# Weights alone on SP's queue behind the first phase, other loads and stores issued by GpSimd

## The chip, the cores and the metric

The kernel runs on one core of a Trainium2 chip. The metric is the device time of the run in microseconds; three runs gave a median of 2641.81 us (2640.67 to 2645.19). One further run was taken with the hardware profiler, and every row quoted below is from it.

## The reference

The reference is a two-layer streaming encoder for one sequence of 512 tokens with 2048 channels, all in float32: first an mLSTM layer (8 heads, key width 256, value width 512), then a layer of banded attention (16 heads of 128) whose keys and values are computed once from the stream between the layers. Both layers are conditioned by a vector c: `sc` is silu(c), and each layer's shift, scale and gate are its product with a matrix of 2048 by 6144, one sum over 2048 entries for each channel.

```python
sc = silu(c)
for l in range(2):
    mod = sc @ ada_w[l] + ada_b[l]
    shift, scale, gate = split(mod, 3)
    h = rmsnorm(x, g_pre[l]) * (1 + scale) + shift
    if l == 0:
        y = mlstm_mixer(h, a_w_in, a_conv_w, a_conv_b, a_gate_b, a_g_head, a_w_out)
    else:
        kmod = sc @ kv_ada_w + kv_ada_b
        hkv = rmsnorm(x, kv_g) * (1 + kmod[D:]) + kmod[:D]
        k, v = split(hkv @ kv_w, 2)
        y = band_attention_mixer(h, k, v, b_w_in, b_rel, b_w_out)
    x = x + gate * rmsnorm(y, g_post[l])
return x
```

Each mixer ends with a product with an output matrix (4096 by 2048 in layer 1, 2048 by 2048 in layer 2).

## The kernel before

Every product of float32 matrices is done as three matmuls (`mm3`, `mm` at L316): both operands are split into a rounded part and a remainder. Activations stay in SBUF as such pairs; weights pass through once. A weight piece is 512 KB in the order in which TensorE needs it. `raw_load` (L260) issues its DMA from SP into one of three slots (`wr`), `wpiece` takes it, ScalarE rounds it into `wh` and VectorE subtracts (`split`, both L244); when VectorE is done the slot is free for the piece three further on. Some pieces also get sums (`ws`, L283 to 285) for products that save a matmul in eight.

The conditioning vectors are not made on TensorE. `ada_load` (L549) brings 128 rows of the transposed matrix (1 MB, or halves of 512 KB) into a slot `ada`, and `ada_sum` (L555) lets VectorE multiply by `sc` and sum along the row into a column of `mod`. They are spread over the kernel: `ada_start` in the first phase (SP), `background` under the mLSTM heads (already issued by GpSimd), `whole_load` under the out-projection of layer 1 (two slots, 1 MB each), `scale_load` (L1226, L1228: tiles `scQ` and `adq`, quarters) under the key projection, `gate_sums` under the out-projection of layer 2 (four slots, half rows).

The stages in order of time: a first phase (input norm, first projections, conditioning sums); gate rows of the mLSTM and eight heads (`ps_qk`, `ps_v`, `ps_o`, `ps_z`; each head loads its rows `nm` and `ssum` from `gsc`, L912 and L913, and stores its output in `ysc`, L1016); the out-projection of layer 1 (`yr` L1067 and L1075, `ps_y_True` and `ps_y_False`, residual rows `xr` L1132 and `xsc` L1141); the normed stream (`nsc`, L1174); the values (`ps_kv`, stores `vsc` L1302 and L1374, each of 512 rows of 512 bytes); the keys (`ksc`, L1366); queries; attention by head (`kt`, `vt` L1394, `bias` L1419, `y2c` L1474); and the out-projection of layer 2 (`y2r` L1529, `ps_y`, tail from about 2500 us), with squares for the output norm (`sqy`, L1116), evictions (`yo`, L1113), the gate columns (`ggd`, stored at L829 and read back as a row at L1105), residuals (`x2`, L1519) and the stores of the result by `finish` (L1543).

`kept` (L1192) loads a normed row (`xt`) back from `nsc` for the sums `hs` and `h2s` that the key and query projections use.

A scheduler with a model of the engines puts each engine's instructions in one order ahead of time, and each engine then runs its queue strictly in that order; an instruction that waits for a semaphore holds everything behind it on that engine, DMA issues included. `pin` keeps calls in the order of the program, and `high_priority` moves some ahead. Before the change SP issues the weights' 537 DMAs and beside them nearly all other loads and stores, GpSimd 57 `ada` loads.

Of the kernel before, what the change touches and what calls it, by code (L numbers as in the profile page):

```python
# [15 lines left out]
P = 128  # L16
D = 2048
S = 512
KT = D // P
# [170 lines left out]
def hybrid_trunk(ctx, tc, xT, xN, c, adaT, cols, wst, wg, ext, kc, out):  # L190
# [351 lines left out]
    def ada_load(i, p, n, pin=lambda ins: ins, parts=1, js=None, queue=nc.sync):  # L542
# [28 lines left out]
    def ada_start(k):  # L571
        return [ada_load(KT + k, ap_, 2, pin), ada_load(k, sp, 2, pin)]
# [14 lines left out]
    early = [ada_load(KT, ap_, 2, pin, 2), ada_load(0, sp, 2, pin, 2)]  # L587
# [98 lines left out]
    def background(n):  # L686
# [4 lines left out]
        while pending and len(loaded) < 3:  # L691
            p, bufs = (bp, 1) if len(pending) % 3 == 1 else (ap_, 2)
            loaded.append(ada_load(pending.pop(0), p, bufs, pin, queue=nc.gpsimd))
# [49 lines left out]
    nc.sync.dma_start(maskd, kc[:, 144:272])  # L743
    graw = tp.tile([P, KT, 16], F32, tag="t", name="graw")
    gw = hp.tile([P, KT, 32], F32R, tag="p0", name="gw")
    nc.sync.dma_start(graw, wg)
# [3 lines left out]
    def gates():  # L750
# [28 lines left out]
        nc.sync.dma_start(gsc[0], on)  # L779
        nc.vector.tensor_tensor(w, u, w, op=ALU.add)  # L780
        nc.scalar.activation(w, w, AF.Exp, scale=-1.0)
        nc.sync.dma_start(gsc[1], w)
# [36 lines left out]
    def gates_out(layer, k0, k1, pl, **kw):  # L819
# [9 lines left out]
        nc.sync.dma_start(ggd[layer, k0:k1], row)  # L829
# [49 lines left out]
    for h in range(NH):  # L879
# [32 lines left out]
        nc.sync.dma_start(nm, gsc[0, h].partition_broadcast(P))  # L912
        nc.sync.dma_start(em, gsc[1, h].partition_broadcast(P))  # L913
# [22 lines left out]
        for i in (2 * h, 2 * h + 1):  # L936
            pin(nc.sync.dma_start(bsc[i], ext[i].partition_broadcast(P)))
# [76 lines left out]
        for i in range(4):  # L1014
            nc.vector.tensor_tensor(so[i], so[i], dd, op=ALU.mult)
            nc.sync.dma_start(ysc[h, :, i, :], so[i])  # L1016
# [23 lines left out]
    def whole_load(bufs=2):  # L1040

        if not scC:
            scC.append(cp.tile([P, D], F32, tag="sc", name=f"scC{whole[0]}"))
            pin(nc.sync.dma_start(scC[0], csc[0].partition_broadcast(P)))
# [15 lines left out]
    def y_tile(k):  # L1060
        while len(ys) <= k:
            n = len(ys)
            h, q = divmod(n // 2, 2)
            with tc.high_priority(AHEAD):
                if n < 4:
                    raw = wp.tile([P, 2, S], F32, tag="raw", name=f"yr{h}_{q}", bufs=RAW_BUFS)
                    nc.sync.dma_start(raw, ysc[h, :, 2 * q : 2 * q + 2, :])  # L1067
                    raw = [raw[:, j, :] for j in range(2)]
                else:
# [4 lines left out]
                    for j in range(2):  # L1074
                        nc.sync.dma_start(raw[j], ysc[h, :, 2 * q + j, :])  # L1075
# [27 lines left out]
    def gate_row(layer, g, gb=ssum):  # L1103

        nc.sync.dma_start(gb, ggd[layer, 4 * g : 4 * g + 4, :].rearrange("k p -> (k p)").partition_broadcast(P))  # L1105
# [22 lines left out]
    def fetch_xr(m, n):  # L1128

        for g in range(len(xrs[m]), len(xrs[m]) + n):  # L1130
            xrs[m].append(xr_p.tile([P, S], F32, tag="xr", name=f"xr{m}_{g}"))
            nc.sync.dma_start(xrs[m][g], xN[m, :, g * S : (g + 1) * S])  # L1132

    def residual(m):
        rs = row_rstd(m)
        for g in range(4):
# [4 lines left out]
            nc.sync.dma_start(xsc[m, :, d], y)  # L1141
# [10 lines left out]
    def turned(pair, gs, use):  # L1152
# [3 lines left out]
        for g in gs:  # L1156
# [5 lines left out]
            for kk in range(2):  # L1162
# [11 lines left out]
                nc.sync.dma_start(nsc[k : k + 2, :, t].rearrange("a p t -> p a t"), keep)  # L1174
# [14 lines left out]
    def kept(k, t):  # L1189
        w = t.stop - t.start  # L1190
        tmp = tp.tile([P, S], F32, tag="t", name=f"xt{k}_{t.start}")[:, :w]
        nc.sync.dma_start(tmp, nsc[k, :, t])  # L1192
# [27 lines left out]
    def scale_load():  # L1220

        for i, j in scale_cols[:2]:
            d = slice(j * S, (j + 1) * S)
            if j not in scQ:
                scQ[j] = cp.tile([P, S], F32, tag="sc", name=f"scQ{j}_{i}", bufs=2)
                pin(nc.sync.dma_start(scQ[j], csc[0, d].partition_broadcast(P)))  # L1226
            a = cp.tile([P, S], F32, tag="adq", name=f"adq{i}_{j}", bufs=4)
            pin(nc.sync.dma_start(a, adaT[i, :, d]))  # L1228
# [61 lines left out]
    def values(g, ms, at={}):  # L1290
        pv = [newp(f"ps_kv{g}_{m}") for m in ms]
        proj_b("kv_w", hkv, pv, ms=ms, at=at)
        for i, (p, m) in enumerate(zip(pv, ms)):
# [8 lines left out]
            nc.sync.dma_start(vsc[g][:, :, m * P : (m + 1) * P], v.rearrange("p (j t) -> p j t", j=4))  # L1302
# [346 lines left out]
```

## Time and profile before

| what | value |
|---|---|
| median of three runs | 2641.81 us |
| the profiled run itself | 2647.62 us |
| span of its records | 2645.8 us |
| TensorE matmul busy | 98% |
| VectorE busy | 89% |
| ScalarE busy | 55% |
| DMA, mean over the span | 193 GB/s |
| packets on SP's queue q1 | 146506, 447.82 MB |
| packets on GpSimd's queue q0 | 8208, 59.77 MB |

The profiled run is one execution, so sums made from its rows are compared with its own 2647.62 us first. Its records span 2645.8 us, and 1.8 us lie outside them. In the rows of waits the columns are the total in us, how often, and the longest; a wait of one engine is named by what ended last. In rows of a timeline or a chain the first number is the start and the second the duration, both in us, and a bracket at the end gives the idle time before. SPq and POOLq are the engines' sequencers, which issue DMAs; PEld is the weight load of TensorE. A row of windows gives each engine's busy time with its instructions, then the granted clock, the share of the DMA engines and GB/s.

### The profile page before, as it was taken

The numbers are of one execution on the slowest core, as the hardware profiler recorded it, in microseconds if no ns is written. First come the engines' busy times: TensorE is split into PE (matmuls) and PEld (weight loads), VectorE is DVE, ScalarE is ACT, GpSimd is POOL, SyncE is SP. The second block draws the span as 40 slices with busy tenths as digits, with TensorE's granted clock in tenths as the row PEclk, the third lists the DMA queues.
The fourth block names the chain that finished last, engine by engine and source line by source line (L and its number), as shares of the span: only waits on it lengthen the run. The fifth ranks groups of instructions, "written<-read, shape, count | busy, mean of one in ns | idle before, by whom it ended". The sixth has DMA issues, their size and how long they took to land.

```text
span 2645.8 us, 45647 instructions
## 1 busy us (share of the span) xinstructions
PE 2581.0 (98%) x17994; PEld 2408.3 (91%) x17994; DVE 2360.7 (89%) x3812; ACT 1461.0 (55%) x2120; POOL 30.6 (1%) x61
## 2 busy tenths in 40 slices
PE   8999999999999999999999999999999999999998
PEld 6887888899999999999999898788999999999887
DVE  8977989999999999999998886977997999999667
ACT  4344533466556566565666443578543776677523
POOL 0000010000000000000000000000000000000000
PEclk9999999999999999999999999999999999999999
DMA  9776797433333333333336648989654544444687
GB/s 366 308 268 234 269 356 295 172 109 127 107 117 108 122 114 116 108 115 122 111 122 221 213 152 304 302 263 306 225 184 137 183 128 143 138 137 136 225 303 255
DMA packets 154929, 510.51 MB, mean 193 GB/s; under 512 B 16549, under 2 KB 30405, under 8 KB 140249
## 3 DMA queue, kind: packets, MB, share of 16 engines
q1 hardware_dynamic: 146506, 447.82, 49.7%
q0 software_dynamic: 8208, 59.77, 6.0%
q8 instruction: 141, 2.31, 0.4%
q14 instruction: 74, 0.61, 0.1%
HBM read 473.92 MB, written 38.85 MB: 194 GB/s over the span
## 4 chain that ended last, share of the span: by engine, by line
PE 51%; DVE 25%; issue 13%; DMA 6%; ACT 4%; POOL 1%; SPq 0%; DVEq 0%; POOLq 0%; ACTq 0%
DVE wh L244 6%; PE ps_azo L316 4%; PE ps_czo L316 4%; PE ps_dzo L316 4%; PE ps_y_False L316 3%; PE ps_y_True L316 3%; PE ps_dz L316 3%; PE ps_cz L316 3%; PE ps_az L316 3%; DVE ada L555 3%; DMA ada<-in_adaT 2%; DMA wr<-in_wst 2%; DVE wsh L244 2%; PE ps_bzo L316 2%; DVE ws L283 2%
## 5 line engine op out<-in xcount | busy, mean ns | idle before, releaser
L244 ACT CAST wh<-wr 128x1024 fp32r<-128x1024 f32 (+1 forms) x536 | 552.8, 1033 | 494.0 <-DVE wr L284 99.3
L244 DVE TENSOR_TENSOR wh<-wr,wh 128x1024 fp32r<-128x1024 f32 (+1 forms) x536 | 642.9, 1202 | 109.5 <-ACT wh L244 108.9
L244 ACT CAST wsh<-ws 128x768 fp32r<-128x768 f32 (+1 forms) x296 | 242.3, 819 | 281.7 <-PE ps_az L316 62.6
L244 DVE TENSOR_TENSOR wsh<-ws,wsh 128x768 fp32r<-128x768 f32 (+1 forms) x296 | 276.3, 933 | 31.7 <-ACT wsh L244 30.6
L555 DVE CUSTOM_DVE_ANT_0 ada<-ada,scB,cl 128x2048 f32<-128x2048 f32 (+1 forms) x89 | 205.9, 2321 | 16.6 <-DMA ada<-in_adaT 16.4
L283 DVE TENSOR_TENSOR ws<-wr 128x512 f32<-128x512 f32 (+1 forms) x296 | 198.1, 673 | 5.3 <-DMA wr<-in_wst 4.9
L316 PE MATMUL ps_y<-wh,y 128*128 128x512 f32 x768 | 171.5, 384 | 4.1 <-ACT sqy L1116 3.5
L316 PE MATMUL ps_y_False<-wh,y 128*128 128x512 f32 x768 | 168.7, 380 | 2.9 <-DVE wh L244 2.9
L316 PEld LDWEIGHTS ps_y<-wh,y 128*128 128x128 f32 x768 | 144.8, 191 | 27.4 <-ACT sqy L1116 4.3
L316 PEld LDWEIGHTS ps_y_False<-wh,y 128*128 128x128 f32 x768 | 144.1, 189 | 25.2 <-DVE wh L244 5.2
L316 PE MATMUL ps_v<-wh,h 128*128 128x512 f32 x576 | 129.2, 383 | 0.0
L316 PE MATMUL ps_kv<-wh,hkv 128*128 128x512 f32 x576 | 126.9, 381 | 1.2 <-DVE wh L244 1.2
L316 PEld LDWEIGHTS ps_v<-wh,h 128*128 128x128 f32 x576 | 109.4, 191 | 16.3 <-issue 0.9
L316 PEld LDWEIGHTS ps_kv<-wh,hkv 128*128 128x128 f32 x576 | 108.0, 189 | 17.7 <-DVE wh L244 2.3
L285 DVE TENSOR_TENSOR ws<-wr 128x256 f32<-128x256 f32 (+1 forms) x296 | 121.5, 414 | 2.9
L284 DVE TENSOR_TENSOR wr<-ws,wr 128x256 f32<-128x256 f32 (+1 forms) x296 | 121.3, 413 | 2.4
L316 PE MATMUL ps_l<-h,wh 128*128 128x512 f32 x480 | 107.7, 380 | 2.1 <-DVE wh L244 2.1
L316 PEld LDWEIGHTS ps_l<-h,wh 128*128 128x128 f32 x480 | 90.2, 189 | 16.6 <-DVE wh L244 3.3
L316 PE MATMUL ps_azo<-h,wh 128*128 128x256 f32 (+1 forms) x606 | 93.0, 285 | 1.8 <-DVE e L865 1.8
L316 PE MATMUL ps_y_True<-wh,y 128*128 128x512 f32 x384 | 83.3, 379 | 0.0
L316 PEld LDWEIGHTS ps_azo<-h,wh 128*128 128x128 f32 x606 | 79.3, 192 | 3.0 <-issue 2.0
L316 PEld LDWEIGHTS ps_y_True<-wh,y 128*128 128x128 f32 x384 | 72.5, 189 | 10.2
(416 smaller groups left out, 5857.3 us busy)
## 6 DMA issues: line engine op xcount, KB each, us to landing
wr<-in_wst SPq DMA_DIRECT2D x506, 512.0 KB, 3.8
ada<-in_adaT POOLq DMA_DIRECT2D x57, 1024.0 KB, 7.3
ada<-in_adaT SPq DMA_DIRECT2D x49, 1024.0 KB, 7.2
ada<-in_adaT SPq DMA_DIRECT2D x36, 512.0 KB, 7.7
wr<-in_wst SPq DMA_DIRECT2D x26, 384.0 KB, 5.6
xt<-nsc SPq DMA_DIRECT2D x32, 256.0 KB, 4.6
yr<-ysc SPq DMA_DIRECT2D x28, 256.0 KB, 5.9
ysc<-zo SPq DMA_DIRECT2D x24, 256.0 KB, 4.4
```

The costliest lines, as they stand in the source:

```text
L244: ins = nc.scalar.copy(hi, src), nc.vector.tensor_tensor(lo, src, hi.bitcast(F32), op=ALU.subtract)
L283: nc.vector.tensor_tensor(t[:, : 2 * w], r[:, w : 3 * w], r[:, : 2 * w], op=ALU.subtract)
L284: nc.vector.tensor_tensor(r[:, w : 2 * w], t[:, w : 2 * w], r[:, :w], op=ALU.add)
L285: nc.vector.tensor_tensor(t[:, 2 * w :], r[:, 3 * w :], r[:, w : 2 * w], op=ALU.subtract)
L316: product[0] = nc.tensor.matmul(ps, a, b, start=start, stop=stop)
L555: pin(nc.vector.tensor_tensor_reduce(c, c, (sc or scB)[:, j * w : (j + 1) * w], 1.0, mod[:, i : i + 1] if j else col(CB + i), ALU.mult, AL ...
```

## The change

From the end of the first phase on, every DMA other than a weight piece is issued by `nc.gpsimd` and no longer by `nc.sync`. The default queue of `ada_load` becomes GpSimd, and the first phase asks for SP by name. The stores of the result for token blocks 2 and 3 stay on SP. No tile, slot count, matmul or sum changes; the scheduler plans the orders anew.

```diff
-    def ada_load(i, p, n, pin=lambda ins: ins, parts=1, js=None, queue=nc.sync):
+    def ada_load(i, p, n, pin=lambda ins: ins, parts=1, js=None, queue=nc.gpsimd):
...
-        return [ada_load(KT + k, ap_, 2, pin), ada_load(k, sp, 2, pin)]
+        return [ada_load(KT + k, ap_, 2, pin, queue=nc.sync), ada_load(k, sp, 2, pin, queue=nc.sync)]
...
-        nc.sync.dma_start(ggd[layer, k0:k1], row)
+        nc.gpsimd.dma_start(ggd[layer, k0:k1], row)
...
-        nc.sync.dma_start(nm, gsc[0, h].partition_broadcast(P))
-        nc.sync.dma_start(em, gsc[1, h].partition_broadcast(P))
+        nc.gpsimd.dma_start(nm, gsc[0, h].partition_broadcast(P))
+        nc.gpsimd.dma_start(em, gsc[1, h].partition_broadcast(P))
...
-                    nc.sync.dma_start(raw, ysc[h, :, 2 * q : 2 * q + 2, :])
+                    nc.gpsimd.dma_start(raw, ysc[h, :, 2 * q : 2 * q + 2, :])
...
-                nc.sync.dma_start(nsc[k : k + 2, :, t].rearrange("a p t -> p a t"), keep)
+                nc.gpsimd.dma_start(nsc[k : k + 2, :, t].rearrange("a p t -> p a t"), keep)
...
-        nc.sync.dma_start(tmp, nsc[k, :, t])
+        nc.gpsimd.dma_start(tmp, nsc[k, :, t])
...
-            nc.sync.dma_start(vsc[g][:, :, m * P : (m + 1) * P], v.rearrange("p (j t) -> p j t", j=4))
+            nc.gpsimd.dma_start(vsc[g][:, :, m * P : (m + 1) * P], v.rearrange("p (j t) -> p j t", j=4))
...
-            nc.sync.dma_start(bias[p0 : p0 + 64, :n], src)
+            nc.gpsimd.dma_start(bias[p0 : p0 + 64, :n], src)
...
-            pin(nc.sync.dma_start(t[i], xsc[m, :, 2 * i * S : 2 * (i + 1) * S].rearrange("p (a t) -> p a t", a=2)))
+            pin(nc.gpsimd.dma_start(t[i], xsc[m, :, 2 * i * S : 2 * (i + 1) * S].rearrange("p (a t) -> p a t", a=2)))
...
-            nc.sync.dma_start(out[m, :, g * S : (g + 1) * S], y)
+            (nc.gpsimd if m < 2 else nc.sync).dma_start(out[m, :, g * S : (g + 1) * S], y)
```

The lines left out do the same for `maskd`, `graw`, `gsc`, `bsc`, `ysc`, `scC`, `yr`, the gate rows, `xr`, `xsc`, `scQ`, `adq`, `ksc`, `kt`, `vt`, `y2c` and `y2r`.

How the queues change is seen in the planned order. In the tail, SP's queue before the change, where the gate columns' half rows (`ada86_0` and on) stand between weights:

```order
L260 DMA wr507_27273<-in_wst 128x1024
L260 DMA wr508_27302<-in_wst 128x1024
L260 DMA wr509_27337<-in_wst 128x1024
L549 DMA ada86_0_27195<-in_adaT 128x1024
L260 DMA wr510_27378<-in_wst 128x1024
L549 DMA ada86_1_27197<-in_adaT 128x1024
L549 DMA ada87_0_27199<-in_adaT 128x1024
L260 DMA wr511_27412<-in_wst 128x1024
L549 DMA ada87_1_27201<-in_adaT 128x1024
L549 DMA ada88_0_27265<-in_adaT 128x1024
L549 DMA ada88_1_27267<-in_adaT 128x1024
L260 DMA wr512_27453<-in_wst 128x1024
```

In the changed kernel SP has the weights alone at that place:

```order
L260 DMA wr507_27273<-in_wst 128x1024
L260 DMA wr508_27302<-in_wst 128x1024
L260 DMA wr509_27337<-in_wst 128x1024
L260 DMA wr510_27378<-in_wst 128x1024
L260 DMA wr511_27412<-in_wst 128x1024
L260 DMA wr512_27453<-in_wst 128x1024
```

and GpSimd's queue has the half rows one behind the other, up to the next gate store:

```order
L1529 DMA y2r7_27139<-y2c7_98 128x1024
L549 DMA ada86_0_27195<-in_adaT 128x1024
L549 DMA ada86_1_27197<-in_adaT 128x1024
L549 DMA ada87_0_27199<-in_adaT 128x1024
L549 DMA ada87_1_27201<-in_adaT 128x1024
L549 DMA ada88_0_27265<-in_adaT 128x1024
L549 DMA ada88_1_27267<-in_adaT 128x1024
L549 DMA ada89_0_27269<-in_adaT 128x1024
L549 DMA ada89_1_27271<-in_adaT 128x1024
L829 DMA ggd_77<-gg1_4_27334 4x128
```

So the half rows no longer stand behind weights, and the weights no longer behind them. The second place is the K/V phase. On SP before, the reloads of normed rows (`xt`), two value stores (`vsc1`) and the first quarters for the scale columns (`scQ`, `adq`) stand between weights:

```order
L1192 DMA xt12_0_18882<-nsc_75 128x512
L260 DMA wr387_19059<-in_wst 128x1024
L1192 DMA xt13_0_18884<-nsc_75 128x512
L260 DMA wr388_19113<-in_wst 128x1024
L1302 DMA vsc1_88<-v1_2_18932 512x1x128
L260 DMA wr389_19180<-in_wst 128x1024
L1302 DMA vsc1_88<-v1_3_18935 512x1x128
L1192 DMA xt14_0_19043<-nsc_75 128x512
L1226 DMA scQ0_76_19225<-csc_76 128x512
L260 DMA wr390_19231<-in_wst 128x1024
L1192 DMA xt15_0_19045<-nsc_75 128x512
L1228 DMA adq76_0_19227<-in_adaT 128x512
```

On GpSimd in the changed kernel the same reloads and stores follow each other:

```order
L1192 DMA xt13_0_18884<-nsc_75 128x512
L1302 DMA vsc1_88<-v1_2_18932 512x1x128
L1192 DMA xt14_0_19043<-nsc_75 128x512
L1302 DMA vsc1_88<-v1_3_18935 512x1x128
L1192 DMA xt15_0_19045<-nsc_75 128x512
L1192 DMA xt0_0_19285<-nsc_75 128x512
L1192 DMA xt1_0_19287<-nsc_75 128x512
L1192 DMA xt2_0_21340<-nsc_75 128x512
L1192 DMA xt3_0_21342<-nsc_75 128x512
L1366 DMA ksc0_79<-zk0_18948 128x1024
L1226 DMA scQ0_76_19225<-csc_76 128x512
L1228 DMA adq76_0_19227<-in_adaT 128x512
```

The weights are on SP's queue alone; each value store stands directly ahead of a reload, and `scQ` and `adq` have moved behind the reloads up to `xt3` and the first key store (`ksc0`).

42 lines of the change are left out of this document (21 added, 21 removed).

## The prediction

> **What bounds the kernel now.** I read the head of the page first, then PE's list of waits, then busy time by stretch, and only then SP's own waits, because the change touches SP's and GpSimd's queues alone and is worth something only where PE ends up waiting for what they carry. All times are us.
>
> ```profile
> PE 2581.0 (98%) x17994; PEld 2408.3 (91%) x17994; DVE 2360.7 (89%) x3812; ACT 1461.0 (55%) x2120; POOL 30.6 (1%) x61
> ```
>
> The span is 2645.8, so PE is idle for 2645.8 - 2581.0 = 65. No edit that leaves the matmuls alone can win more, and the matmul count is unchanged here. PE's waits, over the whole span:
>
> ```profile
> PE ps_cv L316 <- DVE wsh L244: 10.6, 10, 1.3
> ...
> PE ps_n L316 <- DVE so L1004: 3.6, 1, 3.6
> PE ps_y L316 <- ACT sqy L1116: 3.5, 2, 2.7
> ...
> PE ps_z L316 <- DVE wh L244: 3.0, 2, 2.6
> PE ps_y_False L316 <- DVE wh L244: 2.9, 5, 0.7
> ...
> PE ps_dz L316 <- DVE h2s L244: 1.7, 1, 1.7
> ...
> PE ps_dk L316 <- ACT hs L244: 1.2, 1, 1.2
> PE ps_kv L316 <- DVE wh L244: 1.2, 2, 0.8
> ...
> PE ps_dk L316 <- DVE hs L244: 0.3, 1, 0.3
> ```
>
> Columns: total, times, longest. None of these rows names a DMA; where a transfer was late, it shows as a late split (wh, L244) or a late eviction. The largest, ps_cv, is DVE's own arithmetic in the mLSTM heads. By stretch (busy PE, PEld, DVE, ACT, POOL, then clock, share of the DMA engines, GB/s):
>
> ```profile
> 1600.00:1700.00 100.00, 97.11 (x445) 83.16 (x444) 74.14 (x73) 36.64 (x47) 0.00 (x0) 1.00 0.87 309
> 1800.00:1900.00 100.00, 96.62 (x593) 86.51 (x592) 83.36 (x144) 68.53 (x106) 0.00 (x0) 1.00 0.80 266
> ...
> 2100.00:2500.00 400.00, 398.19 (x3264) 389.17 (x3264) 364.45 (x793) 270.56 (x468) 0.00 (x0) 1.00 0.48 152
> 2500.00:2646.00 146.00, 133.20 (x604) 113.48 (x602) 101.07 (x143) 45.33 (x72) 0.00 (x0) 0.98 0.78 267
> ```
>
> Attention (2100 to 2500) leaves PE 1.8 of 400: nothing to win there. Three stretches remain where SP's queue matters: the out-projection of layer 1, the K/V phase, and the tail.
>
> SP's own waits say how much the moved entries held up the weights:
>
> ```profile
> SPq L260 <- DVE wh L244: 1400.1, 397, 10.5
> ...
> SPq L1419 <- DVE mx L1437: 67.9, 15, 4.9
> SPq L549 <- DVE mod L555: 53.8, 24, 4.5
> ...
> SPq L913 <- DVE dd L992: 19.8, 7, 3.3
> ```
>
> The first row is the weights' own: a weight waits till one of its three slots is split. It stays. What the change removes are rows like the last three, where a store or an ada load waits and the weights stand behind it. L1419 (bias) lies inside attention, where PE hardly waits.
>
> **The tail, 2500 on.** This is where the sum comes from. Waits in that stretch:
>
> ```profile
> DVE ada L555 <- DMA ada<-in_adaT: 24.9, 14, 5.6
> ACT wh L244 <- DMA wr<-in_wst: 16.0, 9, 4.5
> ...
> PE ps_y L316 <- ACT sqy L1116: 3.5, 2, 2.7
> ...
> PE ps_y L316 <- DVE wh L244: 0.6, 2, 0.4
> ```
>
> The same stretch's chain of waits and SP's and DVE's instructions (start, duration; a bracket is the idle time before):
>
> ```profile
> 2541.16 1.24 DVE wh L244
> 2543.09 7.44 DMA ada<-in_adaT
> ```
>
> ```profile
> 2542.41 0.33 SPq L260 DMA_DIRECT2D wr<-in_wst  x1
> 2543.09 1.28 SPq L549 DMA_DIRECT2D ada<-in_adaT  x3
> ```
>
> ```profile
> 2533.18 1.28 DVE L555 CUSTOM_DVE_ANT_0 ada<-ada,scC,cl 128x1024 f32<-128x1024 f32 x1 [2.69 <-DMA ada<-in_adaT]
> ...
> 2550.55 1.28 DVE L555 CUSTOM_DVE_ANT_0 ada<-ada,scC,cl 128x1024 f32<-128x1024 f32 x1 [5.56 <-DMA ada<-in_adaT]
> ```
>
> An ada load needs the slot of the sum four loads back. That sum ended at 2533.18 + 1.28 = 2534.5, yet the load left at 2543.09: it stood on SP behind a weight (2542.41), which waited for the split of 2541.16. It took 7.44 to land, DVE stood 5.56 in order, the evictions and squares behind it came late, and PE waited for a bank (the 2.7 of the 3.5). On GpSimd that slot's sum is all that such a load waits for, so it can leave some 8.6 earlier, more than DVE's 5.56. The gate store (ggd, L829) moves ahead of two half loads that it stood behind on SP; it waits for a transpose on PE and a copy on ACT, and meanwhile the half rows still in the four slots cover VectorE. I take the whole row of **3.5 as gained**. The 0.6 for late weights I leave: the same bytes still move. Bounds: a gain of 3.5 + 0.6 = 4.1 at best; at worst none, if the earlier loads only take the same DMA time from the weights (0.78 busy on average), whose lateness already costs ACT 16.0. Issuing costs nothing on the way to the end: the row below gives 534 ns on an engine that is otherwise empty, and SP spent 1.28 on three (above), 0.43 each, of which the weights are rid.
>
> ```profile
> L549 POOL DMA_DIRECT2D ada<-in_adaT x57 | 30.4, 534 | 447.0 <-DVE mod L555 443.9 <-DVE e L875 3.1
> ```
>
> The last eight out stores stay on SP, so the 1.8 between span and the run's time and the end behind the last matmul don't change; the eight that move are done before.
>
> **The K/V phase, 1838 to 1876.** PE waits 1.2 (ps_kv) + 1.2 + 0.3 (ps_dk, for the split of a normed row that was loaded back by L1192) = 2.7. There, 256 KB loads and the stores stand between weights on SP.
>
> ```profile
> L1302 SPq DMA_DIRECT2D vsc<-v x12: 514/525/1478, 1793.0 to 2091.0; - x12
> ```
>
> (minimum, median, maximum ns.) Weights alone on SP would no longer wait for their neighbours; the reloads (xt) now stand on GpSimd each behind a value store of 512 rows. No row shows such a store on GpSimd. From below it costs SP's 525 ns; from above, if the 534 ns is per 128 rows, 4 x 534 = 2.1, an estimate. The order has store, reload, store, reload, so the second reload is at most 2 x 2.1 = 4.3 late. I take 1.0 gained: of the 2.7, the 1.2 of ps_kv are late weights and most of that goes, and the 1.5 of ps_dk stay, for a reload may come earlier for want of weights ahead of it and later for the store. The bounds are 2.7 gained and 4.3 - 1.0, some 3, lost. The same pair of stores ahead of reloads stands at 2043 to 2066, where PE loses 1.7 later (ps_dz); I put it at 0 with the same bound. The quarters for the scale columns move behind the reloads and the first key store, from 1866 to past 1882; their sums come later still (SP's timeline, then the instructions of line 1215):
>
> ```profile
> 1866.29 0.43 SPq L1228 DMA_DIRECT2D adq<-in_adaT  x1
> ...
> 1882.54 0.33 SPq L1366 DMA_DIRECT2D ksc<-zk  x1
> ```
>
> ```profile
> L1215 DVE CUSTOM_DVE_ANT_0 adq<-adq,scQ,cl x4: 743/745/746, 1896.5 to 1910.0; 128x512 f32<-128x512 f32 x4
> ```
>
> That leaves 1896.5 - 1882.9 = 13.6 for a transfer of 256 KB, so 0.
>
> **The out-projection, 1630 to 1700.** PE waits 2.9 in five pieces for wh (above). Is it the order on SP or the bandwidth? 302 GB/s flow at a share of 0.87, and the seven ada loads there show no slot wait ahead of a free weight slot in SP's list. So a split queue brings nothing by itself: 0, bounds from -2.9 to the price of the slower rival below.
>
> **All else.** maskd, graw, the gate stores, nm/ssum, bias, kt/vt, y2c and residual loads wait for the same producers on either engine. In order on GpSimd they stand behind each other, not behind weights; the heads lose PE time to DVE (ps_cv) and attention hardly any. The one 3.6 (ps_n) is a DVE chain. The scheduler re-plans DVE's and PE's order slightly with equal counts: 0, plus or minus 2.
>
> **Sum.** Profiled run: 2647.6 (span 2645.8 + 1.8). -3.5 - 1.0 + 0 + 0 = -4.5, so 2643.1 by that run. The median of the runs is 2641.8, 5.8 below it, and all terms are differences, so I carry them over: **2637.3**, 0.17% faster. A measurement of this kernel can tell about 0.2%, 5.3, from no change: the forecast lies just inside it.
>
> **The rivals.**
>
> *Nothing moves (2641.8).* The slots, not SP, set when weights leave (1400.1 against 53.8), and the tail's transfers are short of bandwidth. For it: 0.78 and 16.0 above. Against: the 5.56 idle while a slot had been free for 8.6. The Trainium skill, DMA: Bandwidth & Descriptors, section Issuing engines are not separate DMA queues, says that all issuers share the same 16 engines and that a second issuer saves only the issuing time. By that rule this rival is the forecast; the trace differs in the tail, where an in-order wait ahead of the issue, not the issue, made the load late.
>
> *More (2632.8).* Every PE gap with a transfer behind it goes: 4.1 + 2.7 + 2.9 = 9.7, less 0.7 for one new gap of the size that those in the out-projection have, 9.0. It needs weights to be early in the DMA-heavy stretches, for which the shares of 0.80 and 0.87 leave little.
>
> *Slower (about 2650).* Ada loads and weights in two queues share the engines, and a weight that used to go out ahead of a 1 MB load now moves beside it. The kernel shows this already in 300 to 480, where ada comes from GpSimd: medians from issue to landing, first in that stretch, then in 1630 to 1700 on one queue:
>
> ```profile
> ada<-in_adaT POOLq DMA_DIRECT2D x37, 1024.0 KB, 7.5
> wr<-in_wst SPq DMA_DIRECT2D x30, 512.0 KB, 6.5
> ```
>
> ```profile
> wr<-in_wst SPq DMA_DIRECT2D x24, 512.0 KB, 4.7
> ada<-in_adaT SPq DMA_DIRECT2D x7, 1024.0 KB, 7.1
> ```
>
> ```profile
> 395.79 1.50 PE L316 MATMUL ps_z<-h,wh 128*128 128x512 f32 x4 [2.63 <-DVE wh L244]
> ```
>
> A weight takes 1.8 longer there and PE once lost 2.63. Where weights are due back to back (1630 to 1700, and the tail with its 14 waits of the sums), each such collision costs 2.63. It decides where more than two of the seven loads of the out-projection, or of the tail's pairs, meet a weight that PE is about to need: then the tail's 3.5 is spent. Five such meetings, 13, less the 4.5 gained, give +8.7, so 2650.5. Against it: in 300 to 480, 37 loads made only 3.0 of PE idle in two pieces. GpSimd's own in-order waits (late xt) end on the same side.
>
> The Trainium skill, SBUF — State Buffer, section Who interferes with whom, has software-generated descriptors held up while DVE runs a two-port mode; that would also be slower. The trace agrees that this kernel's DVE work hardly does it: 57 issues of 534 ns with landing 7.3 against 7.2 from SP (page, below).
>
> ```profile
> ada<-in_adaT POOLq DMA_DIRECT2D x57, 1024.0 KB, 7.3
> ada<-in_adaT SPq DMA_DIRECT2D x49, 1024.0 KB, 7.2
> ```
>
> **How the numbers follow.** Forecast 0.45, nothing 0.20, more 0.13, slower 0.22. Faster by over 0.2%: the 0.13 and the part of the forecast beyond 5.3, some 0.18, together 0.31. Slower by over 0.2%: 0.22 and 0.03 of the others. Within: 0.44. Range: from 2631 (the larger gain with its re-planning) to 2651 (the slower rival), leaving out about 2 in 10.
>
> **What would show it.** Right: in the tail the wait DVE ada <- DMA falls from 24.9 to below 10, no eviction gap of 2.7 on PE, ada loads issued within 1 of the sum that frees the slot; the waits of PE between 1838 and 1876 fall to about 1.7. Wrong: PE <- DVE wh grows beyond 6 between 1600 and 1700 or in the tail, with weights landing at 6.5 and not 4.7 there; ps_dk or ps_dz waits above 3 behind reloads; GpSimd waits longer than 5 ahead of xt.

## The result, and the profile after

The changed kernel takes **2704.95 us** in the median (2700.65 to 2706.24, five runs) against 2641.81 us before (2637.98 to 2645.19, five runs beside it). The ratio is 1.0233, 95% interval 1.0221 to 1.0245: it is slower by 63 us. The profiled run of the changed kernel took 2700.65, that of before 2647.62, so the two traces show 53.1 us of span to be explained (2698.9 against 2645.8).

The head of the page after, engine busy time first and then the two queues (packets, MB, share):

```profile
PE 2602.1 (96%) x17994; PEld 2420.9 (90%) x17994; DVE 2359.8 (87%) x3812; ACT 1458.0 (54%) x2120; POOL 250.4 (9%) x457
...
q1 hardware_dynamic: 84250, 317.00, 33.6%
q0 software_dynamic: 43568, 190.59, 20.9%
```

The transfers moved as the diff says: SP's queue fell from 447.82 to 317.00 MB and GpSimd's rose from 59.77 to 190.59. The count of matmuls is the same, yet PE's busy time rose by 21.1 (2602.1 against 2581.0). The same matmuls took longer, which points at their clock. Only the other 32 of the 53 are added waits.

**Where the time went.** Both kernels issue 17994 matmuls, so the nth matmul of one can be set beside the nth of the other. The growth of the distance between their starts, stage by stage:

| stage (times in the trace of before) | after minus before, us |
|---|---|
| first phase, gate rows, first three heads, to 581 | -1.5 |
| the other five heads, to 1395 | **16.7** |
| end of the heads, `yr` and the next projections, to 1621 | 1.5 |
| out-projection of layer 1, first part, 1621 to 1689 | 4.6 |
| its end, with the stores of normed rows, 1689 to 1752 | **7.5** |
| norm and values, 1752 to 1874 | **14.9** |
| keys and first queries, to 2043 | -0.5 |
| reloads for the queries, 2043 to 2133 | 3.5 |
| attention, to 2447 | 0.2 |
| tail | 6.0 |

Nothing of size was gained anywhere. How far such a number may be trusted is seen from the experiments below, where many stages are built as in one of the two kernels: the start then lies anywhere from -3.3 to 5.6, the heads differ by up to 3, the middle stages by 1 to 3. In the tail, two kernels built there like before show -2.7 and -4.4, so this execution of before was a long one there. Its 2647.62 is 5.8 above its median and the changed kernel's 2700.65 is 4.3 below its own, which is why the traces show 53 and the medians 63.

PE's waits after, over the whole span (total, times, longest), show who pays:

```profile
PE ps_cv L316 <- DVE wsh L244: 16.9, 7, 3.1
...
PE ps_y_False L316 <- DVE wh L244: 7.6, 12, 0.8
...
PE ps_kv L316 <- ACT wh L244: 4.8, 2, 2.9
```

The heads' wait (ps_cv) grew from 10.6 to 16.9, ps_y_False from 2.9 to 7.6, and ps_kv <- ACT wh is new. These are the same late splits as before the change, later still. As before, the row names the split and not the transfer that made it late. That has to be read off the engine that makes the split.

**The heads.** VectorE waits for `nm`. DVE at L914, after and then before (start, duration):

```profile
603.66 0.69 DVE L914 TENSOR_TENSOR nmd<-nm,maskd 128x512 f32<-128x512 f32 x1 [2.32 <-DMA nm<-gsc]
```

```profile
602.66 0.69 DVE L914 TENSOR_TENSOR nmd<-nm,maskd 128x512 f32<-128x512 f32 x1
```

GpSimd's queue in that head, after, and SP's at the same place before:

```profile
596.37 0.54 POOL L913 DMA_DIRECT2D ssum<-gsc  x1 [119.31 <-DVE dd L992]
596.92 0.54 POOL L937 DMA_DIRECT2D bsc<-in_ext  x1
598.35 0.54 POOL L912 DMA_DIRECT2D nm<-gsc  x1 [0.89 <-issue]
```

```profile
597.27 0.33 SPq L913 DMA_DIRECT2D ssum<-gsc  x1
599.02 0.32 SPq L912 DMA_DIRECT2D nm<-gsc  x1
```

The load of `nm` was issued 0.7 earlier than before, and landed later. The medians from issue to landing in 560 to 1420 (before, then after):

```profile
nm<-gsc SPq DMA_DIRECT2D x5, 256.0 KB, 3.2
```

```profile
bsc<-in_ext POOLq DMA_DIRECT2D x10, 320.0 KB, 5.5
...
nm<-gsc POOLq DMA_DIRECT2D x5, 256.0 KB, 5.5
```

So it was not late at issue. It landed with a 320 KB copy, `bsc`, that left 1.4 ahead of it on the same queue; before, `bsc` left some 58 us after `nm`. DVE runs in order, and PE's gap at ps_cv in this head went from 1.24 to 3.10 (DVE is 1.0 later, and PE had come there about 1 earlier by what the first phase won).

**The clock.** What the gap sets off costs more than the gap. PE behind it, after (the head's first matmuls, and the same form 6 us on), and the windows 642 to 648 of after and of before (busy PE, PEld, DVE, ACT, POOL, then clock):

```profile
642.03 0.79 PE L316 MATMUL ps_cv<-wsh,h1s 128*128 128x256 f32 x2 [3.10 <-DVE wsh L244]
...
648.29 0.50 PE L316 MATMUL ps_av<-wh,h1s 128*128 128x256 f32 x3
```

```profile
642.00:648.00 6.00, 5.97 (x28) 5.97 (x29) 6.00 (x10) 2.08 (x4) 0.00 (x0) 0.50 0.25 89
```

```profile
642.00:648.00 6.00, 6.00 (x56) 6.00 (x55) 6.00 (x11) 4.10 (x6) 0.00 (x0) 1.00 0.27 89
```

28 matmuls instead of 56 in the same 6 us, at a granted clock of 0.50. Such a stretch lasts 3.4 or 6.8 us and so costs 1.7 or 3.4. Adding (1 - clock) over all stretches below 0.97, up to the last matmul, gives 6.8 us in 4 stretches before and 23.9 in 10 after: **17 of the 53 us** are matmuls at half clock. The Trainium skill, TensorE: Matmul & The Clock Gate, Part 1: The HAM clock gate, has the clock either half or full, set by a free-running window of about 3.4 us, and puts the fall behind an idle window of that length. The 0.50 and the 3.4 agree. The length of the gap does not: the clock fell behind gaps of 3.10, 2.52 and 1.98 and even behind one of 1.63 (at 2504), and it stayed at full behind gaps of 2.92 and 2.96, and behind most of 1.24 to 1.81.

**The norm and the values.** Two waits of ScalarE grew here, `xk` (L1147) for its own row's store and `xt` (L1326) for the reload. After, ACT around the first, and the matmul behind it; then ACT before:

```profile
1763.57 1.06 ACT L1172 COPY xk<-ps_x 128x512 f32<-128x512 f32 x2
1764.53 1.04 ACT L244 CAST wh<-wr 128x1024 fp32r<-128x1024 f32 x1
1770.24 1.09 ACT L1147 ACTIVATE xk<-xk,mod,amul 128x256 f32<-128x256 f32 x2 [4.67 <-DMA nsc<-xk]
```

```profile
1773.83 0.48 PE L316 MATMUL ps_y_False<-wh,y 128*128 128x512 f32 x1 [1.98 <-ACT wh L244]
```

```profile
1741.84 1.09 ACT L1147 ACTIVATE xk<-xk,mod,amul 128x256 f32<-128x256 f32 x2 [0.93 <-DMA nsc<-xk]
```

ScalarE scales a row in place and so waits till the store that reads the row has gone through; the weight split behind it waits too. With the store on GpSimd that is 4.67 instead of 0.93. Then GpSimd's queue and ScalarE behind it at the first reload:

```profile
1872.24 0.72 POOL L1302 DMA_DIRECT2D vsc<-v  x1 [11.15 <-ACT v L1301]
1872.89 0.60 POOL L1192 DMA_DIRECT2D xt<-nsc  x1
```

```profile
1879.25 0.81 ACT L1326 ACTIVATE xt<-xt,mod,amul 128x512 f32<-128x512 f32 x1 [5.31 <-DMA xt<-nsc]
```

The value store waited 11.15 for its producer, the reload stood behind it and left in the next moment, and ScalarE stood 5.31, with the split that PE then waited for (the 2.9 in ps_kv). Over the run this wait of `xt` is 7.3 in 9 before and 26.0 in 12 after.

### The profile page after: what moved, and what is told of

Read it like the earlier page. It is cut to its first block, busy times and chain, and to the rows that moved or that the text cites. A ratio compares the mean times of both kernels' runs of the same rounds, so it can differ in the third digit from the quotient of the medians.

```text
span 2698.9 us, 45824 instructions
## 1 busy us (share of the span) xinstructions
PE 2602.1 (96%) x17994; PEld 2420.9 (90%) x17994; DVE 2359.8 (87%) x3812; ACT 1458.0 (54%) x2120; POOL 250.4 (9%) x457
## 3 DMA queue, kind: packets, MB, share of 16 engines
q1 hardware_dynamic: 84250, 317.00, 33.6%
q0 software_dynamic: 43568, 190.59, 20.9%
## 5 line engine op out<-in xcount | busy, mean ns | idle before, releaser
L549 POOL DMA_DIRECT2D ada<-in_adaT x108 | 57.6, 533 | 498.3 <-DVE mod L555 480.5
L555 DVE CUSTOM_DVE_ANT_0 ada<-ada,scC,cl 128x2048 f32<-128x2048 f32 (+1 forms) x35 | 65.2, 1862 | 24.0 <-DMA ada<-in_adaT 24.0
```

The lines of the kernel that those rows point to most:

```text
L549: pin(queue.dma_start(at[:, c : c + w], adaT[i, :, j * w : (j + 1) * w]))
L555: pin(nc.vector.tensor_tensor_reduce(c, c, (sc or scB)[:, j * w : (j + 1) * w], 1.0, mod[:, i : i + 1] if j else col(CB + i), ALU.mult, AL ...
```

## The experiments

Most are one of the two kernels with the queue of one or a few lines changed back or moved. "Stage" is the time of a stage above against before's. Every ratio is against the kernel before.

**The heads.** Is the loss the position behind `bsc`, the queue as such, or something else in that stage? The first puts `nm` and `ssum` of the changed kernel on SP:

```diff
-        nc.gpsimd.dma_start(nm, gsc[0, h].partition_broadcast(P))
-        nc.gpsimd.dma_start(em, gsc[1, h].partition_broadcast(P))
+        nc.sync.dma_start(nm, gsc[0, h].partition_broadcast(P))
+        nc.sync.dma_start(em, gsc[1, h].partition_broadcast(P))
```

> The changed kernel, with the two loads of each mLSTM head (nm, L912, and ssum, L913) issued by SP again. In the changed kernel the head's DVE stands 2.3 us until nm has landed (5.5 us after its issue, 3.3 before the change), PE's gap in ps_cv grows from 1.25 to 3.1 us, and the granted clock falls to 0.5 right behind it: about 15 us by the last head. Theory A (the gaps of the heads come from the late nm, and the clock's fall follows the gap): ps_cv gaps back at 1.25, no fall of the clock in the heads, time 12 to 17 us below the changed kernel (about 2689). Theory B (the heads lose time because the scheduler's order of DVE and PE changed, or because GpSimd's descriptors slow DVE): less than 4 us gained, gaps of ps_cv still above 2.

2679.81, ratio 1.0151 [1.0135, 1.0166]: 25 us less than the changed kernel, more than expected. The heads' stage is back at 0.2, `nm` lands in 3.4, and the gaps at ps_cv are 1.23 to 1.48 with no fall of the clock in the heads. That is 16.5 of the 20.7 by which the two traces differ; 2.3 lie in the tail and 1.7 in the start, which is within what differs between runs there.

The second leaves `nm` on GpSimd and takes `bsc` away from its front:

```diff
-            pin(nc.gpsimd.dma_start(bsc[i], ext[i].partition_broadcast(P)))
+            pin(nc.sync.dma_start(bsc[i], ext[i].partition_broadcast(P)))
```

> The changed kernel, with only the copies from DRAM to DRAM (bsc, L937), which stand on GpSimd between the loads ssum and nm of a head, issued by SP. Theory A1 (nm is late since a 320 KB copy stands ahead of it in the same queue): nm lands 3.5 to 4 us after its issue and is issued about 1.5 us earlier, DVE's wait for nm falls below 1 us a head, ps_cv gaps about 1.5 to 2, no fall of the clock in the heads, 8 to 15 us gained over the changed kernel. Theory A2 (a load from GpSimd's queue is itself slower, whatever stands ahead): nm still lands after 5 us or more, gaps of ps_cv about 2.5 to 3, less than 5 us gained.

2685.15, 1.0165 [1.0149, 1.018]. The heads' stage is 2.6, the gaps 1.44 to 2.39, no fall of the clock; `nm` lands in 3.6 in the median. So GpSimd's queue alone is worth some 2.6, `bsc` just ahead of `nm` the other 14. In the heads the orders of PE, VectorE and ScalarE in this trace are those of the changed kernel, so a new plan doesn't explain it.

The third does the heads' moves alone, on the kernel before (`nm`, `ssum` and `bsc` to GpSimd):

> The kernel before, with only nm and ssum (L912, L913) and the copies bsc (L937) of the mLSTM heads issued by GpSimd. If the loss of the heads is made by these three alone: DVE waits about 2.3 us for nm in each of the heads 3 to 7, ps_cv gaps 3 us, the clock falls to 0.5 behind most of them, 13 to 20 us slower than before. If it needs the rest of the moved entries (ysc, ada, the new plan): less than 5 us slower.

2661.27, 1.0084 [1.0065, 1.0103], 19.6 slower than before. The heads' stage is 13.0, with five gaps of 2.92 to 3.10 and three falls of the clock. The part is slow by itself, without the rest of the change. (The two traces differ by only 12.1, since the profiled run of before was a long one; 2.7 of that shows in the tail, where nothing was changed.)

The fourth keeps all on GpSimd and only turns the order, `bsc` behind the head's stores of `ysc`; PE's order is that of the changed kernel, instruction for instruction:

```diff
-        for i in (2 * h, 2 * h + 1):
-            pin(nc.gpsimd.dma_start(bsc[i], ext[i].partition_broadcast(P)))
...
+        for i in (2 * h, 2 * h + 1):
+            pin(nc.gpsimd.dma_start(bsc[i], ext[i].partition_broadcast(P)))
```

> The changed kernel, all queues as they are, with the copies bsc issued behind the head's four ysc stores, so that on GpSimd nm follows ssum directly. Theory A1 (what stands between ssum and nm makes nm late): nm lands 3.3 to 4 us after its issue, DVE waits under 1 us, ps_cv gaps at most 1.8, 13 to 20 us gained over the changed kernel, as with the copies on SP (20 us). Theory A2 (the copies take the DMA engines from nm whoever issues them near it, or GpSimd's loads are slow): under 5 us.

2687.48, 1.018 [1.0165, 1.0195]. The heads' stage fell from 16.7 to 3.7, and the profile shows why (the landing of `nm` in 560 to 1420, then the window that ran at 0.50):

```profile
nm<-gsc POOLq DMA_DIRECT2D x5, 256.0 KB, 3.9
```

```profile
642.00:648.00 6.00, 6.00 (x56) 6.00 (x55) 6.00 (x11) 3.88 (x6) 0.00 (x0) 1.00 0.24 89
```

What costs the time is `bsc` leaving just ahead of `nm`, then: same queues, same bytes, same order on PE, and 13 of 16.7 us gone. One thing isn't separated: whether `bsc` delays `nm` because it is ahead in the same queue, or because both use the DMA engines at that moment, which could happen from two queues as well. In the first kernel `nm` had landed before `bsc` left (26 us after `nm`, in one head 5), in the second `bsc` left 57 us after it. The landing of 3.9 against 3.2 is what GpSimd's queue costs this load with only `ssum` ahead of it, as before.

**The norm and the values.** First all of them at once: `xr`, `xsc`, `nsc`, the first two value stores of a block (L1302) and `xt` back on SP.

```diff
-                nc.gpsimd.dma_start(nsc[k : k + 2, :, t].rearrange("a p t -> p a t"), keep)
+                nc.sync.dma_start(nsc[k : k + 2, :, t].rearrange("a p t -> p a t"), keep)
...
-        nc.gpsimd.dma_start(tmp, nsc[k, :, t])
+        nc.sync.dma_start(tmp, nsc[k, :, t])
...
```

> The changed kernel, with the residual rows (xr, L1132), the stores xsc (L1141), nsc (L1174) and vsc (L1302) and the reloads xt (L1192) issued by SP again; ada, gate rows, heads and attention stay on GpSimd. Theory C (between 1700 and 1900 the stores wait on GpSimd behind other waiting entries, ACT's next copy needs their tiles, and the weight casts behind it on ACT are late): the waits ACT xk <- DMA nsc and ACT xt <- DMA xt fall to the level of before, PE's gaps of 1 us and more between 1760 and 1890 go, 18 to 25 us gained over the changed kernel. Theory D (the stage is short of DMA bandwidth since weights now share the engines with a second queue): the same bytes still move beside the weights, less than 8 us gained.

2685.65, 1.0173 [1.0156, 1.019], 19 us gained. 1689 to 1752 fell from 7.5 to 1.8, and 1752 to 1874 from 14.9 to -1.7. So the loss comes with the move of these DMAs. Weights that land later beside a second queue don't show as the cause: here they land in 4.5 in the median in both traces (1690 to 1876 before, 1690 to 1900 after). Part of it comes back later: 2043 to 2133 shows 6.1 instead of 3.5.

The gate rows (L1105) wait 72.8 us in all on GpSimd (`POOL ssum L1105 <- DVE y L1113`, six times). Do they hold up the stores behind them?

```diff
-        nc.gpsimd.dma_start(gb, ggd[layer, 4 * g : 4 * g + 4, :].rearrange("k p -> (k p)").partition_broadcast(P))
+        nc.sync.dma_start(gb, ggd[layer, 4 * g : 4 * g + 4, :].rearrange("k p -> (k p)").partition_broadcast(P))
```

> The changed kernel, with only the loads of gate rows (L1105) issued by SP. In the changed kernel they wait on GpSimd 72.8 us in all (six times, up to 17.1) for the last eviction, with stores (xsc, nsc) and half rows behind them. Theory C1 (the stage from 1690 to 1900 loses its 25 us because the stores stand behind these waiting loads): the waits of ACT xk and ACT xt for their transfers fall to half or less, 12 to 20 us gained over the changed kernel. Theory C2 (the stores and reloads are late by the queue itself: descriptors, landing, and their own order among each other): less than 5 us gained.

2704.08, 1.0233 [1.0216, 1.025]: nothing, and ACT's wait at L1147 stayed as it was. The stores behind these loads wait for their own rows in any case (`POOL nsc L1174 <- ACT xk L1172`: 32.1 in the changed kernel, 35.7 here). My theory of that wait fell. The next three take one line each back to SP: the row stores `nsc` (L1174), the reloads `xt` (L1192), and all value stores (L1302, L1374).

> The changed kernel, with only the stores of the normed stream (nsc, L1174) issued by SP; the orders of PE and DVE are those of the changed kernel word for word. In the changed kernel ACT overwrites each stored row in place (L1147) and waits for the store, up to 4.7 us with two weight casts behind it. Theory H (each kind of DMA brings its own share, by its own wait on ACT): ACT's waits for nsc fall from 20 to about 10, the PE gap at 1773 goes with the clock's fall behind it, 4 to 8 us gained over the changed kernel. Theory K (it is the planned order alone, so one kind moved back changes nothing): less than 2 us.

> The changed kernel, with only the reloads of normed rows (xt, L1192) issued by SP. In the changed kernel they stand on GpSimd each behind stores, and ACT waits 26 us in all for them, with weight casts behind. Theory H: ACT's waits for xt fall below 10, the PE gaps at 1860 and 1881 (ps_kv, 1.95 and 2.86) go, 7 to 13 us gained over the changed kernel. Theory K: less than 2 us, or the waits move to the next store.

> The changed kernel, with only the value stores (vsc, L1302 and L1374) issued by SP; PE's order is that of the changed kernel. Theory L (the stores of 512 rows are what makes the reloads behind them late, and DVE's norm waits for their tile): the gap of 1.78 at 1814 and those of ps_x go, and the waits for xt fall too, 6 to 12 us gained over the changed kernel. Otherwise the reloads' own queue is what counts: under 4 us.

| back on SP | time | ratio | 1689 to 1752 | 1752 to 1874 | ACT xk L1147 <- DMA nsc | ACT xt L1326 <- DMA xt |
|---|---|---|---|---|---|---|
| all (kernel before) | 2641.81 | 1 | 0 | 0 | 3.8 | 7.3 |
| none (changed kernel) | 2704.95 | 1.0233 | 7.5 | 14.9 | 10.3 | 26.0 |
| `nsc` | 2698.96 | 1.0222 [1.0205, 1.0239] | 1.1 | 12.7 | 4.0 | 22.5 |
| `xt` | 2694.44 | 1.0197 [1.0182, 1.0212] | 6.6 | 9.5 | 10.0 | 16.2 |
| `vsc` | 2694.89 | 1.0204 [1.0189, 1.0219] | 8.7 | 7.7 | 10.2 | 16.0 |

With `nsc` back, PE's and DVE's orders are those of the changed kernel, with `vsc` back PE's is; only the queue differs. Kernels that leave these two stages as the change has them show 6.6 to 8.4 and 12.4 to 15.2. So ScalarE's wait for the row's store is nearly all of the 7.5, and the reload behind the value store a third to a half of the 14.9, whichever of the two is taken away. The other part is gone only with all of them on SP, and what it waits for isn't shown. The rows of the reload say it too: in the changed kernel GpSimd waited 4.4 just before reloads till a value store had landed, and ScalarE waited 26.0 for the reloads; with `vsc` on SP ScalarE waited 16.0:

```profile
  DMA vsc<-v: 4.4, 2
...
  ACT xt L1326: 26.0, 12
```

```profile
  ACT xt L1326: 16.0, 12
```

**The out-projection.** There 1 MB ada loads now run beside the weights. They go back to SP (`whole_load` and `scC`):

```diff
-            pin(nc.gpsimd.dma_start(scC[0], csc[0].partition_broadcast(P)))
-        under_way.append(ada_load(whole.pop(0), cp, bufs, pin))
+            pin(nc.sync.dma_start(scC[0], csc[0].partition_broadcast(P)))
+        under_way.append(ada_load(whole.pop(0), cp, bufs, pin, queue=nc.sync))
```

> The changed kernel, with the 1 MB ada loads of the out-projection of layer 1 (whole_load, L1045, and their row of silu, L1044) issued by SP between the weights again. Theory F (a load of 1 MB that moves beside the weights instead of between them makes each weight late: the prediction's slower rival): PE's waits for wh between 1640 and 1700 fall from 6.1 to about 3, 4 to 6 us gained over the changed kernel. Theory G (the stage is bound by the bytes; only who waits changes): less than 2 us gained.

2702.55, 1.0233 [1.0217, 1.0248]: no net gain. The stage itself did improve, from 4.6 to 1.5 (PE's waits for wh there fell from 6.1 to 2.7), but the one before it went from 1.5 to 5.9, where a gap of 2.18 at 1484 is followed by a fall of the clock; what made that gap isn't shown.

**The tail.** The kernel before, with only the 32 half rows of the gate columns moved to GpSimd (the line issues four at a time), the move on which the prediction's largest term rests:

```diff
-        gate_in[:] = [ada_load(i, op, 4, tc.keep_in_program_order, 2, [j]) for i, j in gate_cols[:4]]
+        gate_in[:] = [ada_load(i, op, 4, tc.keep_in_program_order, 2, [j], nc.gpsimd) for i, j in gate_cols[:4]]
```

> The kernel before, with only the half-row ada loads of the tail (gate_sums, L1558 on) issued by GpSimd. The prediction's term: DVE's wait for ada in the tail falls from 24.9 to below 10, the eviction gap of 2.7 us on PE goes, 3.5 us (with the clock's fall behind that gap up to 5) gained over the kernel before. Theory E (the loads only trade places with the weights on the same DMA engines): the wait of PE for late weights grows as much, no gain, within 2 us of the kernel before.

2642.24 against 2640.87, ratio 1.0006 [0.9995, 1.0016]: no change. Its waits in 2495 to 2641:

```profile
DVE ada L555 <- DMA ada<-in_adaT: 10.9, 8, 3.2
...
ACT wh L244 <- DMA wr<-in_wst: 9.1, 5, 2.3
...
PE ps_y L316 <- ACT sqy L1116: 2.7, 1, 2.7
```

VectorE's wait for ada did fall, from 24.9 to 10.9, and the weights' lateness from 16.0 to 9.1. Each load near the gap left about 0.4 after the sum that frees its slot. PE's gap of 2.7 stayed all the same, because the evictions came late again:

```profile
2533.21 1.28 DVE L555 CUSTOM_DVE_ANT_0 ada<-ada,scC,mod 128x1024 f32<-128x1024 f32 x1 [3.17 <-DMA ada<-in_adaT]
...
2545.44 2.48 DVE L1113 TENSOR_TENSOR yo<-ps_y,ssum 128x512 f32<-128x512 f32 x4
```

```profile
2546.89 1.65 PE L316 MATMUL ps_y<-wh,y 128*128 128x512 f32 x3 [2.65 <-ACT sqy L1116]
```

The evictions (L1113) stand behind sums and weight splits in DVE's order. By the traces 20 of the 32 sums stand ahead of them here, 16 before: the new plan moved four more in front. And an ada load still takes 7.0 to land in the median, so VectorE stood 5.6 for four loads right ahead of the evictions (3.17, 1.06, 1.15 and 0.25). How much is the order and how much the landing isn't separated. Where all half rows and the residual loads stay on GpSimd, in ten of the kernels here, this stage costs 2 to 6; in the two below that give them back, 1.

**Putting it back.** If the named parts explain the loss, the changed kernel with all of them undone should be near the kernel before. GpSimd keeps the rest:

```diff
-        gate_in[:] = [ada_load(i, op, 4, tc.keep_in_program_order, 2, [j]) for i, j in gate_cols[:4]]
+        gate_in[:] = [ada_load(i, op, 4, tc.keep_in_program_order, 2, [j], nc.sync) for i, j in gate_cols[:4]]
...
-            pin(nc.gpsimd.dma_start(t[i], xsc[m, :, 2 * i * S : 2 * (i + 1) * S].rearrange("p (a t) -> p a t", a=2)))
+            pin(nc.sync.dma_start(t[i], xsc[m, :, 2 * i * S : 2 * (i + 1) * S].rearrange("p (a t) -> p a t", a=2)))
...
```

Left out are the lines shown above: `bsc` behind `ysc`, and `nsc`, `xt`, `xr`, `xsc`, `vsc`, the whole ada loads with `scC`, the gate stores and gate rows on SP.

> The changed kernel with all the places that the runs so far blame put right: the copies bsc behind ysc (still GpSimd), and xr, xsc, nsc, xt, vsc, the ada loads of both out-projections with scC of the first, gate stores and gate rows and the tail's residuals on SP. nm, ssum, ysc, yr, the scale columns, ksc and all of attention stay on GpSimd. If these parts add up to the loss (heads 13 of 17, middle 22, both out-projections 10, values to queries 3): 2643 to 2650 us, within 0.3% of the kernel before. If the loss is spread over all moved entries: above 2660.

2660.93, 1.0072 [1.0057, 1.0087]. That places 44 of the 63 us, and misses what I expected: 19.4 are left. 7.0 of them stand in the stage of `yr`, 3.5 in the heads (over all heads VectorE waits 11.0 for `nm` even with `bsc` behind it). Then also `maskd`, `graw`, the gate rows' stores, `nm`, `ssum`, `ysc` and `yr` go back to SP:

```diff
-            nc.gpsimd.dma_start(ysc[h, :, i, :], so[i])
+            nc.sync.dma_start(ysc[h, :, i, :], so[i])
...
-                        nc.gpsimd.dma_start(raw[j], ysc[h, :, 2 * q + j, :])
+                        nc.sync.dma_start(raw[j], ysc[h, :, 2 * q + j, :])
...
```

> As the last kernel (three parts back), with everything else that a compute engine waits for closely on SP too: the gates' loads and stores (maskd, graw, gsc), the heads' nm, ssum and ysc, and yr. GpSimd keeps its 57 ada loads of before, the copies bsc (behind ysc), the scale columns (scQ, adq), ksc, attention (kt, vt, bias, y2c), y2r, scC of the tail and the first eight stores of the result. Theory M (the rest of the loss, 19 us, is spread over the loads that an engine waits for closely, and what stays here is covered by work): 2640 to 2648 us, the same as before. Theory N (any entry on GpSimd costs): above 2655.

2649.72 against 2640.16, 1.0029 [1.0015, 1.0042]: 9.6 left of 63, 4 to 11 by the interval. And the last named part alone, `ysc` and `yr` on the kernel before:

```diff
-                        nc.sync.dma_start(raw[j], ysc[h, :, 2 * q + j, :])
+                        nc.gpsimd.dma_start(raw[j], ysc[h, :, 2 * q + j, :])
...
```

> The kernel before, with only the stores ysc (L1016) and the loads yr (L1067, L1075) issued by GpSimd. With the parts put back the out-projection of layer 1 still began 7 us later than before, with ACT waiting 13.2 us for yr (4.8 before). Theory M: ACT's waits for yr grow to about 13, 4 to 8 us slower than before. Otherwise (that loss comes from ada and the weights on SP there): less than 2 us.

2646.46 against 2640.16, 1.0024 [1.0014, 1.0034]. The stage of `yr` alone shows 7.2, and ScalarE waits there (before, then this kernel):

```profile
ACT y L244 <- DMA yr<-ysc: 4.8, 3, 3.1
```

```profile
ACT y L244 <- DMA yr<-ysc: 13.3, 11, 3.7
```

Again it is a reload that an in-order engine takes up soon after its store. No kernel of these runs is faster than the one before; no part of the change that was tried alone gained anything.

## Why the prediction was wrong

The forecast was 2637.3, the range 2631 to 2651; the time is 2704.95. By the prediction's own steps:

**All else, "0, plus or minus 2": the step that failed.** It said that loads and stores "wait for the same producers on either engine. In order on GpSimd they stand behind each other, not behind weights". The sentence was right and its price was left out; `bsc`, `nsc` and `yr` aren't in its list at all. What a load stands behind matters where an in-order engine takes it up at once. `nm` behind `bsc` cost 13 to 16.5 of the heads' 16.7 (by the kernels with `nm` or `bsc` on SP and with `bsc` later). The prediction had the row ps_cv at 10.6, the largest of PE's waits, and put it down to DVE's arithmetic alone; it didn't ask how soon after the landing of `nm` that arithmetic starts. `yr` cost about 7 when moved alone. The Trainium skill, DMA: Bandwidth & Descriptors, section Queues, rings and completion order, says of the queues of SP and ACT that on each DMA engine descriptors are consumed in ring order. No run here shows whether an order of that kind held `nm` up on GpSimd's queue: it landed in 5.5 with `bsc` just ahead and in 3.9 without, and no kernel has the two leave together from two queues.

**The K/V phase, -1.0 with bounds of 2.7 gained and 3 lost: the term was mis-sized.** Its stretch, 1838 to 1876 in the trace of before, cost 5.4. It asked what the issue of a value store costs on GpSimd, 525 ns to 2.1 us, and that is answered at 0.72 (the row of 1872.24). What it didn't bound is the wait of that store for its own producer, 11.15, behind which the reload stands. The stretch ahead of it, 1689 to 1838, had no term at all and cost 16.9; 7.5 of it is the stage in which ScalarE overwrites `xk` in place behind its store. Rows for both waits were there before the change (`xk` 0.93 at 1741.84; 7.3 in 9 for `xt`). The reloads for the queries, put at 0 with the same bound, cost 3.5.

**The tail, -3.5.** The step from "the load leaves earlier" to "PE's gap goes" failed. The first half is right where it was tried alone (24.9 to 10.9). The second is wrong: VectorE still stood 5.6 for loads right ahead of the evictions, with more sums in front of them. In the changed kernel not even the first half holds:

```profile
DVE ada L555 <- DMA ada<-in_adaT: 25.1, 13, 6.2
...
ACT sqy L1116 <- DVE yo L1113: 14.0, 4, 8.3
```

```profile
PE ps_y L316 <- ACT sqy L1116: 3.6, 1, 3.6
```

25.1 is no less than 24.9, and the gap of 3.6 is still there. The prediction had seen that half rows would now stand behind the gate store (`ggd`), and took it that the rows still in the slots would cover VectorE. They didn't (GpSimd's queue after, then VectorE):

```profile
2577.84 0.53 POOL L829 DMA_DIRECT2D ggd<-gg  x1 [6.81 <-ACT gg L828]
2578.45 2.38 POOL L549 DMA_DIRECT2D ada<-in_adaT  x4
```

```profile
2584.44 1.29 DVE L555 CUSTOM_DVE_ANT_0 ada<-ada,scC,cl 128x1024 f32<-128x1024 f32 x1 [3.67 <-DMA ada<-in_adaT]
```

The first of the four could have left from 2572.8 on, when the sum that frees its slot had ended. A second wait, of 4.65, follows at 2596.95 for a load that left at 2586.14, and then PE's gap. The tail lost 6.0. With the half rows, gate stores, gate rows and residual loads given back it is 1, and with the half rows alone on GpSimd 0.2, which points to what shares the queue with them; how the 6.0 divides is not settled.

**The out-projection, 0 with the rival's price as the bound.** The price fits the rival's kind: 4.6 is about two such meetings of a weight and an ada load and not five, and the stage was back at 1.5 with the ada loads on SP. The meetings themselves are not shown, for weights still landed in 6.2 there (1655 to 1725; 6.5 in the changed kernel). But with them back the loss turned up one stage earlier, so nothing was won by it.

**The rivals.** "Nothing moves" is refuted with the rest. "Slower", at 2650.5, had the right sign but the wrong place: it priced weights that meet ada loads, some 5 us of 63, and only named GpSimd's own in-order waits in half a sentence, without a price, though that was the case that came true. Of the signs listed as wrong, two came: in the out-projection (1655 to 1725) PE waited 6.1 for DVE's `wh` with weights landing in 6.5, and GpSimd waited 11.15 ahead of `xt`. Of those listed as right, the tail's wait below 10 did not come (25.1).

**The multiplier.** No step had the clock in it. Before, 6.8 us were lost to it already, so a gap's price was never its length alone. The change lost 17 more this way; of its 23.9, 10.2 are in the heads, behind gaps that had grown from about 1.25 to about 3.

What stays open: the last 9.6 us of the kernel that keeps only far-off transfers on GpSimd (2.1 lie in the queries' reloads, 1.1 in the tail, and 3.1 in the start, no more than runs differ there); whether `bsc` holds `nm` up in the queue or on the DMA engines; and, in stages where the planned orders of the engines differ too, how much is order and how much queue. For the heads that is settled by the kernel with `bsc` on SP, for `nsc` on PE and DVE and for `vsc` on PE, whose orders were the same.

## What to carry to other kernels

Before transfers are gathered on one queue, ask of each load which instruction takes it up, how long after its landing, and what would stand in front of it: a bulky transfer that nobody needs yet, or a store that waits for its producer, ahead of a load that an in-order engine needs at once, was dearer here than all the waits that the move removed. Move the transfers nobody waits for, or put the urgent one first; here turning one order gave back 13 of 16.7 us. On a kernel that keeps PE busy, price a gap that grows from 1 to 3 us at its growth and, where the clock falls behind it, a further 1.7 or 3.4.

## What the runs showed of the hardware

- In the changed kernel the granted clock fell to 0.50 for 3.4 or 6.8 us behind PE gaps as short as 1.63 and 1.98, and not behind each longer one (2.92 and 2.96 there, two of 3.09 in the kernel with the heads' moves alone). The exact condition stays open.
- A DMA issued by GpSimd occupied it for 0.54 (128 rows) and 0.72 (a value store of 512 rows), against 0.33 and 0.53 on SP, and the 256 KB load `nm`, without `bsc` just ahead, landed in 3.9 instead of 3.2.
- A long wait on the issuing engine by itself said nothing of harm: the largest in the changed kernel, 683.4 us, is `ssum` waiting for `dd`, and taking away another, of 72.8, gained nothing.
